# A two-layer retention / mLSTM trunk on one core: rope tables, squares of x and the silu of c placed anew in the opening

## The chip, the core and the metric

The kernel runs on one core of one Trainium2 chip. The core has five engines that run their own lists of instructions in order: TensorE (PE, matrix products; its weight loads are listed apart as PEld), VectorE (DVE), ScalarE (ACT), GpSimd (POOL) and SyncE (SP), which here only issues loads. Sixteen DMA engines move data for the queues that SP, ACT and POOL feed. The metric is the device time of one launch in microseconds (us); the kernel before took 1474.69 us, the median of three runs (1473.51 to 1475.45).

## The reference, cut to what matters

Sequence length 512, width 1024, batch 1, two layers. Layer 0 mixes tokens by retention with 4 heads, layer 1 by an mLSTM; each is followed by a ConvFFN. What the change touches is the beginning of layer 0: silu of c, the modulation vectors, the first RMSNorm, and the rotary tables that q and k need.

```python
def rmsnorm(x, g):
    xf = x.astype(jnp.float32)
    xn = xf * lax.rsqrt(jnp.mean(xf * xf, axis=-1, keepdims=True) + EPS)
    return xn.astype(x.dtype) * g

def rope(t, positions):
    d = t.shape[-1]
    inv_freq = ROPE_BASE ** (-jnp.arange(0, d, 2, dtype=jnp.float32) / d)
    ang = positions.astype(jnp.float32)[..., None] * inv_freq
    cos = jnp.cos(ang)[:, :, None, :].astype(t.dtype)
    sin = jnp.sin(ang)[:, :, None, :].astype(t.dtype)
    ...

c_act = jax.nn.silu(c)
for i in range(DEPTH):
    mod = c_act @ ada_w[i] + ada_b[i]
    sh_t, sc_t, gt_t, sh_f, sc_f, gt_f = [m[:, None, :] for m in jnp.split(mod, 6, axis=-1)]
    h = rmsnorm(x, norm_tok_g[i]) * (1.0 + sc_t) + sh_t
    ...  # retention or mLSTM of h, its gate, then the ConvFFN with sh_f, sc_f, gt_f
```

## The kernel before

x lies transposed: eight tiles x[0] to x[7] of 128 features by 512 tokens, 256 KB each. All products are float32 made of two parts each: an operand is split into a high part (`whi`, `hh`: a copy that TensorE reads at its fast format) and a low part (`wlo`, `hl`: what is left), and a product is high by high, high by low and low by high.

**The opening** is the function `ret_start`. Its tasks, in the names that the profile shows:

- `c_row` is c as one row; ACT takes its silu; TensorE spreads it to all 128 partitions (`pc`), and two copies write it to `c_ext`. Each modulation column is one instruction on DVE, the function `gemv`: a 128x1025 product-and-sum of a loaded tile `ada` (512.5 KB) with `c_ext`. Column KT+k is the scale, column k the shift of tile k.
- Each x[m] is squared into `sq`; the squares are added up on DVE; the function `means` lets four narrow products per group (`pms` from `sq` and `ones_d`) turn the sums into mean squares of tokens. ACT takes the root into `rc`, DVE the reciprocal, and four products with the unit matrix `eye` spread it to a 128x512 tile.
- For each k from 0 to 7: `scaled` writes `xr` on DVE, ACT writes the high part `hh`, DVE the low part `hl`, and `products(k)` runs 24 products of 128x512 of that tile with the first weight chunk `raw` of `w_s` number k (512 KB; the first head's values and gate), whose high part `whi` ACT copies and whose low part `wlo` DVE subtracts (for k of 5 and more ACT and a POOL transfer make it). For tile 0 `xr` and `hh` are made in two halves.
- Products whose result nobody reads keep TensorE at work while it would wait: `busy(n)` issues n of 128x512 on a constant tile `warm`, `alive(m, w)` one on x[m]. Their counts are the constants `BUSY`, `EXTRA` and `ALIVE`.
- `rope_tables` makes cos and sin from the positions (`posi`: one row of 2 KB, read into all 128 partitions) by some 30 operations on DVE over 128x512 (`ra`, `rk`, `rr`, `rn`) and three on ACT. They are first needed when head 0's q and k are rotated.

**What sets the order.** All instructions are first collected by the class `Plan`. Those issued with `plan.pin` set keep the order of the code on their engine: the opening does, up to the loop over k. All others are listed by a planner that goes by estimated durations, due times counted back from TensorE's list, and the state of the buffers; `plan.soon` gives due times by hand (`ROPE_DUE` is 200), and `.after` or `plan.behind` holds an instruction behind another. The result is a fixed list per engine. A change of the opening therefore also reorders what the planner lists behind it. Loads of SP go out in list order; a load also waits until the buffer it writes and one of eight completion counters are free.

Weights, their parts and the `ada` tiles share 18 buffers of 128x1088, two more take `ada` tiles beside them.

After the loop over k come 96 products `pp` for head 0's q and k, then folded products `p`, scores `psc`, and so on to the end; in these the planner keeps TensorE fed.

## Time and profile before

| | before |
|---|---|
| median of 3 runs | 1474.69 us (1473.51 to 1475.45) |
| profiled execution | 1474.7 us, which is its span from the first to the last instruction |
| TensorE busy | 1458.4 us, 99% of the span |
| VectorE busy | 1289.8 us, 87% |
| ScalarE busy | 1063.3 us, 72% |
| TensorE's mean granted clock | 0.994 of full speed |
| first product that is used (`products(0)`) | 21.06 us after the span's start |

The page gives busy time per engine and the granted clock in 40 slices; the timeline lists instructions in order of time, neighbours of one kind merged, with the start, the time that the row covers, and in brackets the idle time before it and what ended it; the stretches give busy time, clock and DMA rate between two moments. Every number is from one execution, and the timeline's zero is its first instruction. A product on float32 operands shows as two records, so the eight narrow products show as x16.

### The profile page before, as it was taken

To read this page: it belongs to the slowest core of one execution; us is meant where nothing else is said; L and a number is where in the kernel's file an instruction comes from. 1 tells how busy PE (TensorE), PEld (TensorE's weight loads), DVE (VectorE), ACT (ScalarE), POOL (GpSimd) and SP (SyncE) were. 2 spreads that over 40 slices of the span, in tenths; PEclk is the share of its full clock that TensorE was granted. 3 is DMA by queue.
4 is the path that set the end of the run, shared out by engine and by line. 5 is a ranking of instruction groups with operands and counts; after the bars stand their busy time and mean duration, and the time that the engine had idled before them with its cause. 6 is when DMAs were issued, how large, how long until landed. Compare 5 with 4: busy or idle time off the path is not lost.

```text
span 1474.7 us, 27429 instructions
## 1 busy us (share of the span) xinstructions
PE 1458.4 (99%) x10564; PEld 1370.7 (93%) x10564; DVE 1289.8 (87%) x2183; ACT 1063.3 (72%) x1604; POOL 244.5 (17%) x279
## 2 busy tenths in 40 slices
PE   8999999999999999999999999999999999999998
PEld 7889999998999999989999998999989999999997
DVE  7899988887998888889897999999989988886866
ACT  5578768786588676666678985988856877667673
POOL 0313112112011111110001321222121011101010
PEclk8999999999999999999999999999999999999999
DMA  9868988988598999799457875888877678568661
GB/s 365 250 165 218 275 232 234 242 251 208 152 223 210 269 266 253 214 236 248 145 176 172 211 207 183 198 194 196 253 190 193 165 183 206 155 168 206 171 162 59
DMA packets 90822, 306.16 MB, mean 208 GB/s; under 512 B 11954, under 2 KB 14514, under 8 KB 90691
## 3 DMA queue, kind: packets, MB, share of 16 engines
q0 software_dynamic: 29520, 106.97, 38.6%
q1 hardware_dynamic: 60882, 197.18, 38.6%
q8 instruction: 82, 1.34, 0.4%
q10 hardware_dynamic: 288, 0.27, 0.1%
q14 instruction: 50, 0.40, 0.1%
HBM read 195.29 MB, written 2.12 MB: 134 GB/s over the span
## 4 chain that ended last, share of the span: by engine, by line
PE 49%; DMA 1%; ACT 1%; DVE 1%; issue 1%; DVEq 0%; POOL 0%; POOLq 0%
PE p L387 20%; PE po L387 16%; PE pv L387 5%; PE pf L387 3%; PE pav L387 2%; DMA wlo<-wt 1%; PE psc L387 1%; ACT whi L387 0%; PE pp L387 0%; ACT mc L387 0%; DVE sl L387 0%; DVE mc L387 0%; ACT wlo L387 0%; ACT L387 0%; DVE ws L387 0%
## 5 line engine op out<-in xcount | busy, mean ns | idle before, releaser
L387 PE MATMUL p<-hh,whi 128*128 128x256 f32 (+1 forms) x1029 | 284.7, 278 | 1.6 <-DVE p L387 1.5
L387 PE MATMUL p<-hl,whi 128*128 128x256 f32 x1024 | 283.6, 277 | 0.0
L387 PE MATMUL p<-hh,wlo 128*128 128x256 f32 x1024 | 281.6, 278 | 0.1
L387 ACT ACTIVATE wlo<-whi 128x1024 fp32r<-128x1024 f32 (+1 forms) x205 | 215.4, 1055 | 25.6 <-PE po L387 14.7
L387 PEld LDWEIGHTS p<-hh,whi 128*128 128x128 f32 x1029 | 193.9, 188 | 3.0 <-DVE p L387 2.4
L387 PEld LDWEIGHTS p<-hl,whi 128*128 128x128 f32 x1024 | 192.5, 188 | 0.4
L387 PEld LDWEIGHTS p<-hh,wlo 128*128 128x128 f32 x1024 | 191.4, 188 | 0.5 <-DMA wlo<-ws 0.3
L387 PE MATMUL p<-t24h,whi 128*128 128x256 f32 x768 | 170.4, 279 | 2.1 <-ACT fs L387 2.1
L387 PE MATMUL po<-ggl,whi 128*128 128x512 f32 (+1 forms) x448 | 153.1, 343 | 0.0
L387 PE MATMUL po<-ggh,whi 128*128 128x512 f32 (+1 forms) x448 | 152.0, 344 | 0.7 <-ACT whi L387 0.7
L387 PE MATMUL po<-ggh,wlo 128*128 128x512 f32 (+1 forms) x448 | 152.5, 343 | 0.0
L387 PE MATMUL p<-t24l,whi 128*128 128x256 f32 x512 | 142.1, 277 | 0.0
L387 DVE SCALAR_TENSOR_TENSOR x<-po,mod,x 128x512 f32<-128x512 f32 (+1 forms) x184 | 113.6, 628 | 30.7 <-PE po L387 29.8
L387 ACT CAST whi<-raw 128x1024 fp32r<-128x1024 f32 (+1 forms) x113 | 113.5, 1015 | 32.6 <-PE po L387 8.4
L387 PEld LDWEIGHTS p<-t24h,whi 128*128 128x128 f32 x768 | 130.4, 188 | 4.9 <-ACT fs L387 2.5
L387 DVE SCALAR_TENSOR_TENSOR cv<-p,vecs,cv 128x511 f32<-128x511 f32 (+1 forms) x152 | 111.2, 743 | 12.0 <-ACT cv L387 11.7
L387 DVE SCALAR_TENSOR_TENSOR ada<-ada,c_ext 128x1025 f32<-128x1025 f32 x96 | 117.6, 1227 | 0.3 <-DMA ada<-ada 0.3
L387 PE MATMUL po<-yl,whi 128*128 128x256 f32 (+1 forms) x352 | 115.3, 328 | 0.0
L387 PE MATMUL po<-yh,whi 128*128 128x256 f32 (+1 forms) x354 | 115.3, 328 | 0.0
L387 PE MATMUL po<-yh,wlo 128*128 128x256 f32 (+1 forms) x352 | 115.3, 328 | 0.0
L387 POOL DMA_DIRECT2D wlo<-wa x55 | 47.5, 864 | 366.3 <-ACT wlo L387 207.7
L387 ACT CAST whi<-ws 128x1024 fp32r<-128x1024 f32 x88 | 92.0, 1048 | 20.7 <-DVE ws L387 13.6
(292 smaller groups left out, 4394.6 us busy)
## 6 DMA issues: line engine op xcount, KB each, us to landing
ada<-ada SPq DMA_DIRECT2D x96, 512.5 KB, 6.6
wlo<-ws POOLq DMA_DIRECT2D x61, 512.0 KB, 7.6
wlo<-wa POOLq DMA_DIRECT2D x55, 512.0 KB, 6.5
wlo<-wt POOLq DMA_DIRECT2D x45, 512.0 KB, 7.5
wa<-w_up SPq DMA_DIRECT2D x38, 512.0 KB, 5.6
wb<-w_up SPq DMA_DIRECT2D x38, 512.0 KB, 8.9
wlo<-raw POOLq DMA_DIRECT2D x34, 512.0 KB, 8.2
raw<-w_o SPq DMA_DIRECT2D x32, 512.0 KB, 7.8
```

The lines of the kernel that those rows point to most:

```text
L387: getattr(c.obj, c.name)(*[real(v) for v in c.a], **{key: real(v) for key, v in c.k.items()})
```

## The change

In the opening:

- `posi` is no longer loaded by ACT's queue at the start but by SP's, behind the first `hh`, after the second part of `vecs`. All of `rope_tables` is issued there too; before, its first five operations came ahead of everything else in the opening, and two more before the first `xr`.
- ACT takes the silu of c first, with one table load ahead; the load of the root's table moves behind the last copy to `c_ext`. Both copies to `c_ext` are now ACT's.
- x[0], x[1] and x[6] are squared on DVE, the others on ACT. The means are formed of three groups (tiles 0 to 3, 4 and 5, 6 and 7) instead of two, so DVE adds five times instead of six.
- Unread products: 7 before the first wait, one on each of x[1], x[3], x[4], x[5], x[6], then 2, 3 and 4 on `warm`, in place of 6, four on x, 4, 3 and 6.
- On SP the first weight chunk goes ahead of the second `ada` tile, and the second ahead of the fourth.

```diff
-BUSY = (6, 1, 1)
-EXTRA = (4, 2, 5)
-ALIVE = (0, 0, 256, 256, 256, 256, 0, 0)
-SUMMED = 6
+FILLS = (7, 2, 3, 4)
...
-    A.dma_start(posi[:], pos.broadcast_to([P, T]))
...
-        plan.soon, tables = ROPE_DUE, rope_tables()
-        next(tables)
-        plan.soon, plan.pin = None, uid("pin")
+        plan.pin = uid("pin")
         A.activation(rc[:, :1], eps_t[:], AF.Silu)
         A.activation(c_row[:1, :], c_row[:1, :], AF.Silu)
-        A.activation(rc[:, :1], eps_t[:], AF.Sqrt)
-        busy(BUSY[0])
-        for i in range(2):
-            PE.matmul(pcs[i][:], one, c_row[:1, i * T : i * T + T], start=True, stop=True)
...
         load_ada(KT)
+        load_raw(0)
         load_ada(0)
-        load_raw(0)
         load_ada(KT + 1)
+        load_raw(1)
         load_ada(1)
-        load_raw(1)
...
+        busy(FILLS[0])
+        square(0, "DVE")
+        square(1, "DVE")
+        square(2)
+        add(0, 1)
+        alive(1, 256)
+        for i in range(2):
+            PE.matmul(pcs[i][:], one, c_row[:1, i * T : i * T + T], start=True, stop=True)
+        square(3)
+        add(1, 2)
+        alive(3, 256)
+        square(4)
+        alive(4, 256)
+        add(2, 3)
+        square(5)
+        means(3, True)
         A.copy(c_ext[:, :T], pcs[0][:])
+        add(4, 5)
+        alive(5, 256)
+        square(6, "DVE")
+        alive(6, 256)
+        means(5, False)
+        square(7)
+        add(6, 7)
+        A.copy(c_ext[:, T : 2 * T], pcs[1][:])
+        busy(FILLS[1])
+        means(7, False)
+        A.activation(rs[:, :1], eps_t[:], AF.Sqrt)
+        busy(FILLS[2])
         gemv(0, KT, mod[KT])
         gain(0, 0, 0)
         A.activation(rc[:, :4], ps[:, :4], AF.Sqrt, bias=eps_t[:])
         high(0)
         V.reciprocal(rc[:, :4], rc[:, :4])
...
+        gemv(0, 0, mod[0])
+        busy(FILLS[3])
         xr = xrs[0] = slot("xr")
...
         S.dma_start(vecs[:, VEC["nffn"] :], vec[:, VEC["nffn"] :]).after = first
+        S.dma_start(posi[:], pos.broadcast_to([P, T])).after = first
+        plan.soon, plan.behind = ROPE_DUE, first
+        for _ in rope_tables():
+            pass
+        plan.soon, plan.behind = None, None
         for k in range(KT):
             ...
                 high(k + 1)
+                plan.calls[-1].after = first
```

TensorE's list from its first product to the first used one (`whi` with `hh`), before:

```order
L387 MATMUL pst_117<-warm_97,ones_81 128x512 x6
L387 MATMUL pc_148<-c_row_99,ones_81 128x512
L387 MATMUL pc_166<-c_row_99,ones_81 128x512
...
L387 MATMUL pst_117<-x_127,ones_81 128x256
L387 MATMUL pst_117<-warm_97,ones_81 128x512 x4
L387 MATMUL pms_211<-ones_d,sq_194 128x1 x4
L387 MATMUL pms_211<-ones_d,sq_200 128x1 x4
L387 MATMUL pst_117<-warm_97,ones_81 128x512 x3
L387 MATMUL pms_211<-eye_134,rc_110 128x128 x4
L387 MATMUL pst_117<-warm_97,ones_81 128x512 x6
L387 MATMUL pst_117<-whi_228,hh_252 128x512
```

and now:

```order
L384 MATMUL pst_115<-warm_97,ones_81 128x512 x7
L384 MATMUL pst_115<-x_110,ones_81 128x256
...
L384 MATMUL pms_199<-ones_d,sq_164 128x1 x4
L384 MATMUL pst_115<-x_125,ones_81 128x256
L384 MATMUL pst_115<-x_129,ones_81 128x256
L384 MATMUL pms_199<-ones_d,sq_178 128x1 x4
L384 MATMUL pst_115<-warm_97,ones_81 128x512 x2
L384 MATMUL pms_199<-ones_d,sq_188 128x1 x4
L384 MATMUL pst_115<-warm_97,ones_81 128x512 x3
L384 MATMUL pms_199<-eye_133,rc_106 128x128 x4
L384 MATMUL pst_115<-warm_97,ones_81 128x512 x4
L384 MATMUL pst_115<-whi_220,hh_238 128x512
```

The means now come in three groups with unread products between them; between the last group and the first used product stand 3, the spread of `rc`, and 4.

ScalarE's list from the root of the means to the high part of tile 1. `whi` is written from the chunks `raw` of `w_s`; `hh_252` and `hh_238` belong to tile 0, `hh_303` and `hh_294` to tile 1. Before:

```order
L387 ACTIVATE rc_110<-pms_211,eps_t 128x4
L387 CAST whi_228<-raw_141 128x1024
L387 CAST whi_238<-raw_154 128x1024
L387 ACTIVATE hh_252<-xr_249,mod_86 128x256 x2
L387 COPY rs_259<-pms_211 128x512
L387 CAST whi_275<-raw_168 128x1024
L387 ACTIVATE hh_303<-xr_295,mod_86 128x512
L387 CAST whi_309<-raw_178 128x1024
```

and now:

```order
L384 ACTIVATE rc_106<-pms_199,eps_t 128x4
L384 CAST whi_220<-raw_138 128x1024
L384 ACTIVATE hh_238<-xr_233,mod_86 128x256 x2
L384 COPY rs_193<-pms_199 128x512
L384 CAST whi_254<-raw_146 128x1024
L384 CAST whi_263<-raw_162 128x1024
L384 CAST whi_276<-raw_174 128x1024
L384 ACTIVATE hh_294<-xr_286,mod_86 128x512
```

Before, three chunks were copied ahead of tile 1's high part; now all of the first four are, the fourth (`raw_174`) directly ahead of it, and none but the first ahead of tile 0's.

SyncE's list between `eye` and the fourth chunk, now:

```order
L384 DMA ada_135<-ada 128x1025
L384 DMA raw_138<-w_s 128x1024
L384 DMA ada_140<-ada 128x1025
L384 DMA ada_144<-ada 128x1025
L384 DMA raw_146<-w_s 128x1024
L384 DMA ada_151<-ada 128x1025
L384 DMA ada_153<-ada 128x1025
L384 DMA ada_160<-ada 128x1025
L384 DMA raw_162<-w_s 128x1024
L384 DMA ada_167<-ada 128x1025
L384 DMA ada_171<-ada 128x1025
L384 DMA raw_174<-w_s 128x1024
```

The fourth chunk was the twelfth of these loads before the change too; only chunks 0 and 1 moved forward by one place each.

More of the change, by code (lines that the diff above doesn't have):

```diff
@@ L1686, in alive, with square @@
         def alive(m, w):
-            if w:
-                PE.matmul(pss[0][:, :w], ones["1"][:].bitcast(F32), x[m][:, :w], start=True, stop=True,
-                          skip_group_check=True)
-        square(0)
-        A.copy(c_ext[:, :T], pcs[0][:])
-        V.tensor_copy(c_ext[:, T : 2 * T], pcs[1][:])
-        for m in range(1, KT):
-            square(m)
-            if m != SUMMED:
-                add(m - 1, m)
-            else:
-                busy(EXTRA[0], free=EXTRA[0])
-                means(m - 1, True)
-            alive(m, ALIVE[m])
-        means(KT - 1, False)
+            PE.matmul(pss[0][:, :w], ones["1"][:].bitcast(F32), x[m][:, :w], start=True, stop=True,
+                      skip_group_check=True)
+        def square(m, eng="ACT"):
+            sq[m] = slot("sq")
+            if eng == "ACT":
+                A.activation(sq[m][:], x[m][:], AF.Square)
+            else:
+                V.tensor_tensor(sq[m][:], x[m][:], x[m][:], op=ALU.mult)
+        busy(FILLS[0])
[14 more added lines that the diff above has]
+        means(3, True)
+        A.copy(c_ext[:, :T], pcs[0][:])
+        add(4, 5)
[10 more added lines that the diff above has]
+        busy(FILLS[2])
         gemv(0, KT, mod[KT])
@@ L1707, in ret_start @@
         V.reciprocal(rc[:, :4], rc[:, :4])
-        pin, plan.pin, plan.soon, plan.behind = plan.pin, None, ROPE_DUE, len(plan.calls) - 1
-        for _ in tables:
-            pass
-        plan.pin, plan.soon, plan.behind = pin, None, None
-        gemv(0, 0, mod[0])
-        busy(BUSY[1] + EXTRA[1], free=EXTRA[1])
         for t in range(4):
```

5 lines of the change are left out of this document (2 added, 3 removed).

## The prediction

> **What bounds the kernel now.** I read the page first: the engines' shares and the granted clock, then the timeline of the first 30 us by engine, then the stretches and the DMA queues.
>
> ```profile
> span 1474.7 us, 27429 instructions
> PE 1458.4 (99%) x10564; PEld 1370.7 (93%) x10564; DVE 1289.8 (87%) x2183; ACT 1063.3 (72%) x1604; POOL 244.5 (17%) x279
> PEclk8999999999999999999999999999999999999999
> ```
>
> TensorE is busy all the time and at full clock but in the first slice. What an opening can give is therefore the distance to the first used product, and only as far as TensorE stays fed from there. The timeline of that distance:
>
> ```profile
> 1.31 2.93 PE L387 MATMUL pst<-warm,ones 128*128 128x512 f32 x6 [1.31 <-POOL warm L387]
> 4.17 1.98 PE L387 MATMUL pc<-c_row,ones 1*128 1x512 f32 x4
> 7.68 3.60 PE L387 MATMUL pst<-x,ones 128*128 128x256 f32 x8 [1.52 <-DMA x<-xT]
> 13.09 2.42 PE L387 MATMUL pms<-ones_d,sq 128*128 128x1 f32 x16 [0.88 <-DVE sq L387]
> 16.80 1.91 PE L387 MATMUL pms<-eye,rc 128*128 128x128 f32 x8
> 20.64 1.16 PEld L387 LDWEIGHTS pst<-whi,hh 128*128 128x128 f32 x4
> 21.06 1.16 PE L387 MATMUL pst<-whi,hh 128*128 128x512 f32 x4
> 26.59 1.07 PE L387 MATMUL pst<-whi,hh 128*128 128x512 f32 x4
> ```
>
> The means end at 15.51, tile 0's products start at 21.06, tile 1's at 26.59: one tile takes 5.53 us. From there TensorE runs without a gap for 62 us:
>
> ```profile
> 26.60:89.00 62.40, 62.40 (x287) 52.13 (x286) 57.87 (x110) 40.68 (x61) 18.34 (x13) 1.00 0.82 246
> ```
>
> So **26.59 is the moment to beat**, not 21.06. Who feeds tile 1:
>
> ```profile
> 4.10 1.28 ACT L387 ACT_TABLE_LOAD   x1
> 18.69 1.04 ACT L387 CAST whi<-raw 128x1024 fp32r<-128x1024 f32 x1 [1.88 <-DMA raw<-w_s]
> 19.64 0.90 ACT L387 ACTIVATE hh<-xr,mod 128x256 fp32r<-128x256 f32 x2
> 22.46 1.05 ACT L387 CAST whi<-raw 128x1024 fp32r<-128x1024 f32 x1 [1.45 <-DMA raw<-w_s]
> 24.72 0.73 ACT L387 ACTIVATE hh<-xr,mod 128x512 fp32r<-128x512 f32 x1 [1.20 <-DVE xr L387]
> 26.32 1.05 ACT L387 CAST whi<-raw 128x1024 fp32r<-128x1024 f32 x1 [0.88 <-DMA raw<-w_s]
> ```
>
> Three times ACT waits for a chunk of `w_s` to land: number 1 at 18.69, 2 at 22.46, 3 at 26.32. Tile 1's `hh` ran between chunks 2 and 3 and was done at 25.45, 1.1 us early.
>
> **The change part by part.** *Loads of x.* DVE waits for the positions until 6.32, SP cannot issue the last x until they land, and the engines move little meanwhile:
>
> ```profile
> 6.32 0.43 DVE L387 CAST ra<-posi 128x512 f32<-128x512 int32 x1 [4.93 <-DMA posi<-pos]
> 8.56 0.69 DVE L387 COPY c_ext<-pc 128x512 f32<-128x512 f32 x1
> 9.16 4.47 DVE L387 TENSOR_TENSOR sq<-sq,sq 128x512 f32<-128x512 f32 x6
> 17.12 0.69 DVE L387 TENSOR_TENSOR rk<-rk,rk 128x512 f32<-128x512 f32 x1
> 17.84 0.43 DVE L387 TENSOR_SCALAR rk<-rk 128x512 f32<-128x512 f32 x1
> 18.74 0.87 DVE L387 SCALAR_TENSOR_TENSOR xr<-x,gain,pms 128x256 f32<-128x256 f32 x2 [0.47 <-PE pms L387]
> SPq L387 <- DMA posi<-pos: 1.8, 1, 1.8
> DMA packets 539, 0.79 MB, mean 187 GB/s; under 512 B 159, under 2 KB 159, under 8 KB 539
> q1 hardware_dynamic: 276, 0.52, 38.8%
> q10 hardware_dynamic: 263, 0.27, 34.1%
> DMA packets 1011, 1.74 MB, mean 405 GB/s; under 512 B 113, under 2 KB 214, under 8 KB 1011
> ```
>
> The first of the two packet rows is the stretch 1.8 to 6.0 us with its queues below it (q10 is ACT's: `vecs` and the positions), the last row 6.0 to 10.3; the DVE rows between are for the parts below. In 4.2 us 0.79 MB moved; at the later 405 GB/s it would be 1.70 MB. Without the positions at least their own 0.27 MB go, 0.67 us; at most the shortfall goes too, (1.70 - 0.79) / 0.405 = 2.25 us, together 2.9 us. I take 2.2 us, nearer the upper end: the shortfall lasts as long as the positions do, but the first x would still have to ramp up. So each later load lands some 2.2 us earlier, 0.67 to 2.9.
>
> *TensorE to the first used product.* Its list is now dense. From 1.31: 7 fills at 2.93 / 6 = 0.49 us, 3.4; one x product at 3.60 / 4 = 0.90 at half clock or half that, `pc` 1.98, two x products 0.9 to 1.8; so about 8 us. Then three groups of means at 2.42 / 2 = 1.21, two x products, two fills: 5.5 to 7.5 more. The means end at 13.5 to 15.5, against 15.51. From there it took 5.55 us; the copy of chunk 1, which held `hh` from 18.74 + 0.87 / 2 = 19.2 to 19.64, is gone, and the last fills are two fewer, so about 5.0. Squares and sums don't set this: on DVE five sums and three squares at 4.47 / 6 = 0.75 us are 6.0 us, most of it while the x still land. The root's table load (the row at 4.10, 1.28 us) costs nothing either, as it runs on ACT while the last sum and the last means run (0.75 + 1.21, behind two fills). If that cover went, it would add 1.28. The first used product starts at 18.5 to 20.5, say 19.0: 2 us earlier. The 5.53 us of tile 0 are done at 24.5.
>
> *Tile 1.* Here ACT's new list decides. `hh` of tile 1 now stands directly behind the copy of chunk 3, which ACT cannot start before that chunk lands. Chunk 3 is the twelfth load behind `eye` in both lists, so it only gains what x gained: 26.32 - 2.2 = 24.1. The copy hands over 0.95 later (18.69 to 19.64), `hh` takes 0.73, TensorE's weight load follows some 0.1 behind (20.54 to 20.64). Tile 1's products start at 26.32 + 0.95 + 0.73 + 0.1 - 2.2 = **25.9, 0.7 us earlier than 26.59**; with 2.9 it is 25.2, with 0.67 it is 27.4, 0.8 later. Whatever the opening gains beyond that is spent waiting for this chunk: TensorE idles from 24.5 to 25.9. A check by bytes: x, `eye` and the twelve loads are 8.46 MB, 20.9 us at 405 GB/s, from about 2 us on; the chunk cannot land before 23.
>
> *The clock.* A gap in TensorE's work has a price of its own:
>
> ```profile
> 6.00:8.00 2.00, 0.48 (x2) 0.33 (x2) 1.58 (x4) 1.57 (x4) 0.00 (x0) 0.89 1.05 404
> 10.00:12.00 2.00, 2.00 (x8) 1.48 (x6) 1.79 (x3) 1.46 (x3) 0.00 (x0) 0.76 1.06 422
> 12.00:14.00 2.00, 1.12 (x9) 0.92 (x9) 1.90 (x4) 0.00 (x0) 0.00 (x0) 1.00 1.04 424
> 14.00:16.00 2.00, 2.00 (x12) 1.90 (x12) 1.09 (x5) 0.39 (x2) 0.00 (x0) 0.60 1.01 410
> 20.00:22.00 2.00, 2.00 (x7) 1.58 (x7) 2.00 (x4) 1.01 (x3) 0.00 (x0) 0.70 1.03 422
> ```
>
> First number behind the stretch's length is TensorE's busy time, the third from the end the granted clock. Read as steps between 1.0 and 0.5, the clock falls at 7.6, rises at 11.0, falls at 14.4, rises at 21.2: multiples of 3.4 us apart. Both falls follow a gap (1.52 us, 0.88 us) and thin work. Those edges continue at 24.6, 28.0, 31.4. A gap of 1.4 us before tile 1 can cost nothing, one step (half speed for up to 3.4 us, 1.7 lost) or, as from 14.4 to 21.2, two. Bounds 0 and 3.4; I take 0.9, as a fall is about as likely as none. The Trainium skill ("TensorE: Matmul & The Clock Gate", Part 1) has a free-running window of 3413 ns, which the spacing bears out, and advises against idle gaps above about 3.4 us; by that advice alone this gap would cost nothing and the sum would be 0.9 lower, yet here the clock fell after gaps of 1.52 and 0.88 us.
>
> *Rope tables.* Seven operations, five from 6.32 to 8.56 and two from 17.12 to 18.27, 3.4 us together, move from the opening to the stretch where DVE is full:
>
> ```profile
> 50.00:60.00 10.00, 10.00 (x46) 8.29 (x45) 7.20 (x14) 6.10 (x7) 0.86 (x1) 1.00 0.98 291
> 60.00:80.00 20.00, 20.00 (x90) 16.58 (x89) 20.00 (x39) 15.04 (x26) 13.00 (x7) 1.00 0.55 125
> 80.00:100.00 20.00, 18.85 (x131) 17.28 (x130) 20.00 (x41) 15.23 (x28) 2.64 (x3) 1.00 0.73 198
> 83.00 0.63 ACT L387 ACTIVATE rk<-rr 128x512 f32<-128x512 f32 x1 [1.96 <-DVE rr L387]
> 90.06 0.37 ACT L387 COPY fs<-p 128x256 f32<-128x256 f32 x1
> 90.48 0.39 PE L387 MATMUL p<-t24h,whi 128*128 128x256 f32 x1 [1.06 <-ACT fs L387]
> ```
>
> TensorE's one wait there, 1.06 us, hangs on `fs`, 7 us behind the tables' end on ACT. DVE has 2.8 us free between 50 and 60, which hides most of the move. Bounds: -1.06 (the wait vanishes, as fewer copies now stand between the tables and `fs`) and +3.4 (the cover is gone). I take +0.3. The positions themselves, now read at about 27 us, delay the loads behind them by 0.7 to 2.9 us; chunk 3 was copied at 26.32 and is used two tiles after 26.59, at 37.6, and the later ones have the same lead, so nothing.
>
> **Sum**, against the profiled execution's 1474.7, which is the runs' median (1474.69): 1474.7 - 0.7 + 0.9 + 0.3 = **1475.2 us**.
>
> **The rivals.**
> - *The clock holds* through the gap. For it: a gap in the middle of dense work, split by an edge, may leave both sides busy enough. Against it: the two falls above. 1475.2 - 0.9 = 1474.3. The skill's advice would have this one.
> - *x is not faster than its bytes allow*: something other than the positions holds the first loads. For it: the queues' rows show both queues slow in one stretch, not which held which. Against it: the rate doubles once the positions are in. Then tile 1 starts at 27.4, the gap is longer and costs a full step: 1474.7 + 0.8 + 1.7 + 0.3 = 1477.5.
> - *DVE becomes the bound* between 58 and 107 us: the moved 3.4 us find no free time, because DVE's list waits for chunks anyway, and the stretch ends that much later than before in absolute time whatever the opening gave. It decides once the delay exceeds DVE's lead over TensorE there; 83.00 to 90.48 says that lead is thin for `fs` only. 1474.7 + 3.4 = 1478.1, slower.
> - *The change does what it says*: the first product is 3 to 4 us earlier and nothing is given back. That needs chunk 3 to land before 21.5, against the bytes. 1474.7 - 3.5 = 1471.2.
>
> **How the numbers follow.** Forecast 0.55, clock holds 0.20, x not faster 0.10, DVE bound 0.09, full gain 0.06. About 0.2% (2.95 us) is what a measurement of this kernel can tell from no change. Faster by more than that: the last case, 0.06. Slower by more (above 1477.6): the DVE case, half of the third and a tail of two clock steps in the forecast, 0.09 + 0.05 + 0.02 = 0.16. The same: 0.78. The range reaches from 1473.0 (clock holds, full 2.9 us, no wait for `fs`: 1474.7 - 1.4 - 0.3) to 1477.6; the forecast's own is 1473.8 to 1476.8.
>
> **What would show it.** In the changed profile: x squared from before 5 us and the last square before 9.5; the means' last group ended before 15.5; the first used product at 18.5 to 20.5; ACT's fourth copy of `raw` waiting for DMA until about 24, `hh` of tile 1 behind it, a gap on TensorE ended by that `hh`, tile 1 at about 25.9, and a half clock in part of 24 to 32. Wrong it would be if ACT does not wait at that copy, if tile 1 starts before 24, or if TensorE shows new gaps between 60 and 110 us.

## The result, and the profile after

The changed kernel takes 1482.2 us, the median of six runs (1480.6 to 1485.35), against 1475.07 for six runs of the kernel before (1472.9 to 1480.1): ratio 1.0051, 95% interval 1.0037 to 1.0065. **It is slower by 0.5%, and the forecast of 1475.2 with its range of 1473.0 to 1477.6 does not hold it.** The profiled execution took 1485.35 us, the longest of the six; its span is 1483.6, 8.9 more than before.

TensorE's opening, as the timeline of the changed kernel has it:

```profile
1.32 3.35 PE L384 MATMUL pst<-warm,ones 128*128 128x512 f32 x7 [1.32 <-POOL warm L384]
4.50 1.22 PE L384 MATMUL pst<-x,ones 128*128 128x256 f32 x2
5.66 3.78 PE L384 MATMUL pc<-c_row,ones 1*128 1x512 f32 x4
9.37 2.08 PE L384 MATMUL pst<-x,ones 128*128 128x256 f32 x4
11.24 1.71 PE L384 MATMUL pms<-ones_d,sq 128*128 128x1 f32 x8
12.80 2.05 PE L384 MATMUL pst<-x,ones 128*128 128x256 f32 x4
14.65 1.71 PE L384 MATMUL pms<-ones_d,sq 128*128 128x1 f32 x8
16.22 1.20 PE L384 MATMUL pst<-warm,ones 128*128 128x512 f32 x2
17.22 1.70 PE L384 MATMUL pms<-ones_d,sq 128*128 128x1 f32 x8
23.62 1.54 PE L384 MATMUL pst<-whi,hh 128*128 128x512 f32 x4
29.55 1.07 PE L384 MATMUL pst<-whi,hh 128*128 128x512 f32 x4
```

There is no gap from 1.32 on. The durations tell the clock: `pc` takes 3.78 us for the same two products (four records) that took 1.98 before, a group of means 1.71, and the first four products of use 1.54 against 1.07 for the next such four. TensorE ran at half clock until some 24.6 us: such a row of four takes 2.08 us at half clock (lean_hand, below) and 1.07 at full, so 1.54 means that the first 0.9 us of it were at half. (The profile's row of granted clocks has nothing to show there, since its records begin with the first change of the clock.) Tile 1 starts at 29.55 instead of 26.59: 3.0 us late.

Nobody else is late. DVE's last sum of squares and ACT's root, in the same kernel:

```profile
3.73 1.44 DVE L384 TENSOR_TENSOR sq<-x 128x512 f32<-128x512 f32 x2 [2.34 <-DMA x<-xT]
10.11 0.69 DVE L384 TENSOR_TENSOR sq<-sq,sq 128x512 f32<-128x512 f32 x1
19.31 0.18 DVE L384 RECIPROCAL rc<-rc 128x4 f32<-128x4 f32 x1 [6.88 <-ACT rc L384]
19.02 0.26 ACT L384 ACTIVATE rc<-pms,eps_t 128x4 f32<-128x4 f32 x1 [7.03 <-PE pms L384]
23.94 2.95 ACT L384 CAST whi<-raw 128x1024 fp32r<-128x1024 f32 x3
28.13 0.72 ACT L384 ACTIVATE hh<-xr,mod 128x512 fp32r<-128x512 f32 x1 [1.24 <-DVE xr L384]
```

The sums are done at 10.80 us, 2.8 earlier than before (13.6), and then DVE and ACT wait 7 us for TensorE's means. The three chunk copies run back to back, without a wait for a load.

The other part of the loss lies far behind the opening. TensorE's busy time by stretches, first the kernel before, then the changed one:

```profile
85.00:150.00 65.00, 63.85 (x500) 62.03 (x499) 61.71 (x106) 51.34 (x87) 16.92 (x23) 1.00 0.81 203
150.00:250.00 100.00, 99.51 (x740) 94.53 (x740) 88.39 (x135) 72.78 (x110) 20.16 (x22) 1.00 0.96 259
250.00:300.00 50.00, 50.00 (x409) 48.87 (x408) 42.97 (x70) 40.51 (x62) 10.13 (x12) 1.00 0.77 200
300.00:340.00 40.00, 38.93 (x283) 36.70 (x282) 34.51 (x58) 32.33 (x52) 5.72 (x12) 1.00 0.83 237
```

```profile
85.00:150.00 65.00, 63.45 (x480) 60.79 (x479) 62.30 (x108) 49.56 (x83) 15.98 (x20) 1.00 0.77 192
150.00:250.00 100.00, 98.49 (x724) 93.07 (x723) 90.21 (x136) 72.78 (x113) 19.88 (x24) 1.00 0.94 252
250.00:300.00 50.00, 49.56 (x404) 48.85 (x404) 39.14 (x62) 38.30 (x58) 10.15 (x11) 1.00 0.86 224
300.00:340.00 40.00, 36.95 (x284) 35.88 (x283) 31.41 (x50) 29.37 (x47) 6.52 (x12) 0.96 0.88 240
314.60:318.00 3.40, 3.40 (x16) 3.40 (x17) 3.31 (x6) 1.43 (x3) 0.33 (x1) 0.52 1.03 339
```

Length less busy time is TensorE's idle time. Before it is 1.15 + 0.49 + 0 + 1.07 = 2.7 us, after 1.55 + 1.51 + 0.44 + 3.05 = 6.55: 3.8 more. The last row shows in addition 3.4 us at half clock, right behind the longest wait, 1.7 us lost. So 3.0 + 3.8 + 1.7 = 8.5 of the 8.9.

The same can be read off one product. The first `po` behind the `pav` products near 340 us stands behind the place where TensorE's lists agree again; in the kernel before, in the change, and in after_again, a second profile of the change:

```profile
341.30 0.39 PE L387 MATMUL po<-yh,whi 128*128 128x512 f32 x1
351.53 0.39 PE L384 MATMUL po<-yh,whi 128*128 128x512 f32 x1
348.40 0.39 PE L384 MATMUL po<-yh,whi 128*128 128x512 f32 x1
```

It is 10.2 and 7.1 us late, which is 7.3 and 7.0 more than tile 1 is (3.0 and 0.1). So the stretch between costs some 1.8 us more than idle time and half clock account for (5.5 and 5.2); where these lie the profiles do not say. Behind this product TensorE's list is the same in all kernels below, and yet the rest took 1123 to 1129 us in their profiles. That 8.5 comes so near to 8.9 is in part chance: the change had made good 1.4 us of its 10.2 at the last product.

The longest of the waits, on TensorE and on ACT's list:

```profile
312.16 0.28 PE L384 MATMUL p<-hh,wlo 128*128 128x256 f32 x1
314.59 0.48 PE L384 MATMUL p<-t24h,whi 128*128 128x256 f32 x1 [2.15 <-ACT fs L384]
312.70 1.06 ACT L384 ACTIVATE wlo<-whi 128x1024 fp32r<-128x1024 f32 x1 [1.59 <-PE p L384]
313.66 0.60 ACT L384 CAST whi<-wb 128x512 fp32r<-128x512 f32 x1
314.17 0.36 ACT L384 COPY fs<-p 128x256 f32<-128x256 f32 x1
```

TensorE needs the copy `fs` before it may go on, and in ACT's list that copy now stands behind a `wlo` that waits for TensorE to free its buffer, and behind a cast. The angle tables were long done by then (their last operation on DVE starts at 87.2 us). What is left of their move at 300 us is the order that the planner found after it: TensorE's list differs from that of before up to some 290 us, ACT's to some 370.

### The profile page after: what moved, and what is told of

Read it like the earlier page. It is cut to its first block, busy times and chain, and to the rows that moved or that the text cites. A ratio compares the mean times of both kernels' runs of the same rounds, so it can differ in the third digit from the quotient of the medians.

```text
span 1483.6 us, 27429 instructions
## 1 busy us (share of the span) xinstructions
PE 1466.1 (99%) x10571; PEld 1375.9 (93%) x10571; DVE 1292.1 (87%) x2184; ACT 1061.5 (72%) x1602; POOL 236.3 (16%) x279
## 4 chain that ended last, share of the span: by engine, by line
PE 83%; DVE 5%; DMA 5%; ACT 3%; issue 2%; POOL 0%; DVEq 0%; POOLq 0%; ACTq 0%
PE p L384 35%; PE po L384 26%; PE pv L384 7%; PE pav L384 4%; PE pst L384 3%; PE pf L384 3%; DMA wlo<-wt 2%; DMA wlo<-wa 2%; PE pp L384 2%; PE psc L384 2%; ACT whi L384 1%; PE pc L384 1%; DVE ws L384 1%; DMA wb<-w_up 1%; DMA wlo<-ws 1%
```

## The experiments

Theory A: two causes that add, TensorE's own opening list and the lists re-planned behind it. Rivals: B, the tables' place alone; C, the opening alone; D, DVE's full stretch at 70 to 106 us sets its own end. "Idle" is TensorE's idle time from 85 to 340 us, and "`po` late" how much later than before the `po` product starts, both as above and from each kernel's one profiled execution. None of them leaves out anything that the output needs.

"Of before" holds for TensorE's list from the first used product on. On ACT and DVE a few instructions still stand in another place up to some 80 us, so that "instruction for instruction" in the expectation of tables_early is not quite so: before, DVE's `rr` at 52.93 us stands ahead of `xr` at 53.53; in tables_early it is behind it, 60.72 and 60.06. Only delay_only has every list of before.

| kernel | lists behind the opening | tile 1 at | `po` late | idle | ratio to before (95%) |
|---|---|---|---|---|---|
| before | its own | 26.59 | | 2.7 | |
| the change | re-planned | 29.55 | 10.2 | 6.55, half clock 3.4 us | 1.0051 (1.0037 to 1.0065) |
| after_again (the change) | the same | 26.69 | 7.1 | 6.2, half clock 3.4 us | 1.0052 (1.0034 to 1.0070) |
| ten_fills | the same | 26.84 | 7.0 | 6.6 | 1.0060 (1.0042 to 1.0077) |
| after_fs | the same but two | 27.08 | 4.8 | 5.25 | 1.0053 (1.0037 to 1.0069) |
| tables_late | re-planned otherwise | 28.40 | 3.5 | 4.4 | 1.0023 (1.0012 to 1.0034) |
| lean | re-planned otherwise | 23.27 | 2.6 | 6.0, half clock 3.4 us | 1.0010 (0.9998 to 1.0023) |
| tables_early | of before | 31.82 | 5.4 | 2.9 | 1.0029 (1.0018 to 1.0039) |
| after_idle | of before | 32.17 | 5.4 | 2.3 | 1.0032 (1.0018 to 1.0046) |
| after_hand | of before | 29.27 | 4.2 | 2.8 | 1.0032 (1.0017 to 1.0046) |
| after_hand_late | of before but five | 28.02 | 9.7 | 2.8 | 1.0032 (1.0018 to 1.0046) |
| lean_idle | of before | 31.63 | 4.1 | 1.8 | 1.0043 (1.0030 to 1.0056) |
| lean_five_late | of before but five | 29.29 | 5.7 | 4.9 | 1.0042 (1.0026 to 1.0058) |
| lean_idle_few | of before | 30.20 | 3.1 | 2.0 | 1.0030 (1.0014 to 1.0045) |
| lean_hand | of before | 27.78 | 3.9 | 2.1 | 1.0034 (1.0021 to 1.0048) |
| lean_hand_hh | of before but three | 25.23 | 6.6 | 1.85 | 1.0053 (1.0039 to 1.0067) |
| delay_only | of before | 28.14 | 1.1 | 2.2 | 1.0007 (0.9996 to 1.0019) |

**tables_early: the changed opening with the tables where they stood.**

Against the changed kernel:

```diff
     A.dma_start(vecs[:, : VEC["nffn"]], vec[:, : VEC["nffn"]])
+    A.dma_start(posi[:], pos.broadcast_to([P, T]))
...
-        plan.pin = uid("pin")
+        plan.soon, tables = ROPE_DUE, rope_tables()
+        next(tables)
+        plan.soon, plan.pin = None, uid("pin")
...
         V.reciprocal(rc[:, :4], rc[:, :4])
+        pin, plan.pin, plan.soon, plan.behind = plan.pin, None, ROPE_DUE, len(plan.calls) - 1
+        for _ in tables:
+            pass
+        plan.pin, plan.soon, plan.behind = pin, None, None
...
-        S.dma_start(posi[:], pos.broadcast_to([P, T])).after = first
-        plan.soon, plan.behind = ROPE_DUE, first
-        for _ in rope_tables():
-            pass
-        plan.soon, plan.behind = None, None
```

> The changed opening, but the positions load on ACT's queue and the angle tables stand where they stood before; behind the opening every engine's list is then the list of before, instruction for instruction. Theory A (two causes: TensorE's own opening list, which ran at half clock until 24.5 us in the changed profile and put tile 1 at 29.55 instead of 26.59, and the lists behind the opening, re-planned by the moved tables, which cost the rest between 150 and 330 us): tile 1 again at 29 to 31 us, half clock up to there, no added waits of TensorE from 90 to 330 us beyond the 2.1 us for fs and 0.4 us for p of before; 1475.1 + 3 to 4 = 1478 to 1479. Rival B (the tables' place alone costs it all): tile 1 near 26.6, time 1475. Rival C (the opening's delay costs it all, and what stood behind it in the profile was chance): 1481 to 1482.

1480.45 us, ratio 1.0029: 4.3 over before (2.7 to 5.8), a little more than A's 3 to 4 and under the 6 to 7 that C asked for. B is out: the tables stood in their old place. Tile 1 came at 31.82, 2.3 later than in the change, because the loads of x come late again; the idle time, 2.9, is that of the old lists, as A has it, and `po` is 5.4 late where tile 1 was 5.2: nearly nothing is added between.

**tables_late: only positions and tables moved.**

Against the kernel before (the second half of the tables behind the reciprocal is taken out likewise):

```diff
-    A.dma_start(posi[:], pos.broadcast_to([P, T]))
-        plan.soon, tables = ROPE_DUE, rope_tables()
-        next(tables)
...
+        S.dma_start(posi[:], pos.broadcast_to([P, T])).after = first
+        plan.soon, plan.behind = ROPE_DUE, first
+        for _ in rope_tables():
+            pass
+        plan.soon, plan.behind = None, None
```

> The kernel before, with only the positions' load and the angle tables moved to behind tile 0, as in the change; squares, silu order, groups of means and fills as before. Theory A: x lands about 2 us earlier, TensorE's opening list stays the old one, so tile 1 is no later than 26.6, perhaps 1 to 2 us earlier if ACT does not wait for a chunk; but the lists behind the opening are re-planned (TensorE's up to about 320 us) and cost some 4 us there: 1477 to 1479 if tile 1 stays, 1476 at best. Rival B (tables' place costs it all): 1480 to 1482. Rival C (only the opening costs): 1473 to 1475.

1479.12 us, 3.4 over before (1.8 to 5.0), at A's upper end; B asked for 1480 to 1482, C for 1473 to 1475. The profile shows how the early loads are wasted in that opening:

```profile
4.18 2.19 PE L387 MATMUL pc<-c_row,ones 1*128 1x512 f32 x4
10.94 1.95 PE L387 MATMUL pms<-ones_d,sq 128*128 128x1 f32 x16 [1.27 <-DVE sq L387]
20.79 2.08 PE L387 MATMUL pst<-whi,hh 128*128 128x512 f32 x4 [4.75 <-ACT hh L387]
```

The means end at 12.9, 2.6 earlier than before. But the planner changed the opening too: on DVE a third modulation column now stands ahead of `xr` (before, it stood behind it, at 20.66) and waits 3.99 us for its load, TensorE idles 4.75 us, and then the first products run at half clock (2.08 for four): tile 1 is 1.8 us later than before, and the re-planned lists add 4.4 - 2.7 = 1.7 of idle time. Together 3.5, as `po` has it, and near the 3.4 of the times.

**lean and ten_fills: less and more on TensorE's opening list.**

Against the changed kernel; in lean the other four calls of `alive` go too. First lean, then ten_fills:

```diff
-FILLS = (7, 2, 3, 4)
+FILLS = (7, 0, 3, 4)
...
-        alive(1, 256)
```

```diff
-FILLS = (7, 2, 3, 4)
+FILLS = (10, 2, 3, 4)
```

> The changed kernel without the ten products on x that nothing reads and without the two fills between the means' second and third group; first fills 7, later ones 3 and 4 as in the change. The lists behind the opening are re-planned once more. Theory A: the last sum is done at 10.8 us as in the changed profile, the last means right behind it at about 11.7, and with the 4.7 us from there to the first product of use this starts at 16 to 17 us, 7 us earlier than in the change; half clock for one more stretch of 3.4 us costs 1.7, tile 1 at 23 to 25. Then 1482.2 - 5 to -6 = 1476 to 1477 if the lists behind the opening cost the same, and whatever is under 1475 shows that they do not. Rival L (loads or DVE set the opening, not TensorE's list): first product not before 21, tile 1 not before 27, 1480 or more.

> The changed kernel with 10 fills instead of 7 at the start; every other instruction of every engine is the same, in the same order. Asks whether the half clock is what makes TensorE's list late, or the list's length. Half-clock theory: three more fills (1.5 us) fill the stretch in which the clock is decided, full clock comes for at least one 3.4 us stretch before 15 us, the rows of pc, x and means shrink to half there, first product of use at 22 to 23.6, time 1481 to 1482. Length theory: no full clock before 24, first product at 25, time 1483.5 to 1484.

lean took 1477.06 us. Its opening, in the timeline:

```profile
4.44 1.98 PE L384 MATMUL pc<-c_row,ones 1*128 1x512 f32 x4
7.73 5.34 PE L384 MATMUL pms<-ones_d,sq 128*128 128x1 f32 x24 [1.32 <-DVE sq L384]
17.78 1.12 PE L384 MATMUL pst<-whi,hh 128*128 128x512 f32 x4
23.27 1.09 PE L384 MATMUL pst<-whi,hh 128*128 128x512 f32 x4
```

Five unread products on x (ten records in the timeline; the expectation counts these) and two fills fewer, and the first product of use is 5.8 us earlier than in the change's profile: TensorE's list set the opening, not loads, DVE or ACT. Part of that is the clock, since `pc` took 1.98 us here; lean_hand, below, had its `pc` at 3.78 as the change had, and its first product at 18.13. Of the 3.3 us that tile 1 is ahead of the kernel before nothing is left, since idle time of 6.0 us and one fall of the clock follow (-3.3 + 3.3 + 1.7 = 1.7; measured +1.4 in the medians, 1.5 by the ratio, -0.3 to 3.4).

In ten_fills the profile and the times disagree. In the profiled execution, the shortest of its six runs (1482.1), the half-clock theory holds: `pc` 2.36, first product of use at 21.36, 2.3 us earlier than in the changed kernel's profile in spite of three more fills. Its median of 1484.42 is 2 us over the change, as the length theory has it. after_again, below, shows that one and the same list can have either clock. Whether more fills bring the full clock more often is not shown, and by its interval ten_fills can't be told from the change.

**after_idle, lean_idle, lean_five_late, lean_idle_few: positions in the opening's idle time, first attempt.**

Against the changed kernel (after_idle) or against lean (the other three); the second half of the tables stands behind the reciprocal, as in tables_early.

```diff
         load_raw(1)
+        S.dma_start(posi[:], pos.broadcast_to([P, T]))
...
+        tables = rope_tables()
+        next(tables)
         gemv(0, KT, mod[KT])
```

In lean_five_late five of the seven operations are then moved in the finished list, ahead of the next angle operation; lean_idle_few has fewer fills:

```diff
-FILLS = (7, 0, 3, 4)
+FILLS = (7, 0, 1, 2)
```

> The whole changed opening (its squares, silu order, three groups of means, products on x that nothing reads, fills), but the positions are read on SP behind the second chunk of w_s, and the first seven angle operations stand in the stretch of the opening in which DVE waits for the means (12.2 to 19.3 us in the changed profile). Behind the opening all lists are those of before. Theory A (two causes that add): the opening's price stays, tile 1 at 29 to 30 us, and the price of the re-planned lists goes; the waits of TensorE between 200 and 330 us are back at before's 0.5 and 1.1 us; 1475.6 + 3 = 1478 to 1479, 3 to 4 under the change. Rival C (the opening alone costs): 1481 to 1482.

> As the run before, but without the ten unread products on x and without the two fills ahead of the means' last group. Theory A: tile 1 at 23.3 to 24, 3 us earlier than before, with the lists of before behind it; whatever of that survives the stretch in which DVE is full (70 to 106 us) is the gain: 1472.3 if all of it, 1474.5 if DVE's list there ends as late as before. Rival D (DVE's full stretch and the loads set its end whatever the opening gives): 1475 to 1476, no gain. In either case 2 to 4 under the run lean, which differs in the place of the tables alone.

> As lean_idle, but five of the seven angle operations (0.43 + 0.89 + 0.69 + 0.43 = 2.4 us of DVE) are taken out of the opening and put directly ahead of the next angle operation, at some 50 us; no other instruction changes its place on any engine. Separates DVE's work from the re-planned lists. DVE theory (what the moved tables cost is DVE's time in its full stretch): 1.5 to 2.4 over lean_idle, with new waits of TensorE between 80 and 110 us. Lists theory (the cost is in the order that the planner then finds, above all between 200 and 340 us): within 0.7 of lean_idle.

> As lean_idle, with one fill instead of three ahead of the rc broadcast and two instead of four ahead of the first product of use. In the profile of lean the broadcast could start at 13.7 and starts at 14.37, and hh is there 0.3 us before the last fill ends; so the first product comes 0.7 to 1.1 us earlier if the fills are what it waits for. Against that the clock: fewer fills may leave the half clock in place for one stretch of 3.4 us more, 1.7 us lost. By the first 0.5 to 1 under lean_idle, by the second 0.7 to 1 over it.

These failed as openings, through an error of mine. DVE's timeline of lean_idle:

```profile
17.81 0.43 DVE L384 CAST ra<-posi 128x512 f32<-128x512 int32 x1 [6.43 <-DMA posi<-pos]
21.46 0.17 DVE L384 RECIPROCAL rc<-rc 128x4 f32<-128x4 f32 x1
```

Issued at 9.33 on SP, the positions landed 8.3 us later, behind everything that SP had issued; the cast waits for them, the reciprocal stands behind the cast, and tile 1 comes at 29 to 32 us. lean_idle_few, 0.5 under lean_idle in the medians, says nothing of fills for the same reason. What they do tell: with the old lists the idle time is 1.8 to 2.3 us however late TensorE is. lean_five_late is the exception. TensorE is 2.3 us earlier there than in lean_idle, and 1.42 us of idle time appear in 85 to 150, most of it one wait of 1.29 for `fs` at 94 us: in the old order five late operations of DVE do cost TensorE time in that stretch, as the DVE theory has it (after_hand, below, where TensorE is as late and two operations are, has 0.12 there). The two medians (1480.4, 1480.76) are alike, so what DVE's work costs in time is not settled.

**after_hand, after_hand_late, lean_hand: second attempt.** Planned as after_idle and lean_idle; then a few instructions are moved in the finished list, and nothing else: the positions on SP ahead of the first chunk, two angle operations ahead of the reciprocal, three ahead of `xr`, two ahead of the next angle operation (in after_hand_late five there).

```diff
-        for n in self.order():
+        out = self.order()
+        for late, ahead in self.moves:
+            out = [n for n in out if n not in late]
+            at = min(out.index(n) for n in ahead)
+            out[at:at] = late
+        for n in out:
```

> What after_idle was meant to be: the positions landed there at 17.6 us, 8.3 after their issue, and the reciprocal stood behind their first operation on DVE. Now the whole changed opening, the positions read on SP ahead of the first chunk of w_s, two angle operations between gain and the reciprocal, three behind the second gemv, two directly ahead of the next angle operation at some 50 us; every list behind the opening is that of before. Theory A (the opening costs 3 us, the lists re-planned for the late tables the other 4): tile 1 at 29.5 to 30.2, no wait over 1.1 us between 200 and 330 us, 1475 + 3 = 1478. Theory C (the opening alone): 1481 to 1482.

> As after_hand, but five of the seven angle operations (2.4 us of DVE) directly ahead of the next angle operation at some 50 us, all else in its place. DVE theory: DVE's full stretch from 70 to 106 us ends 2.4 later, TensorE was already 3 late there and waits for what is left: 0.5 to 2.4 over after_hand. Lists theory: the same as after_hand within 0.7, and so 3 under the change.

> The same places of positions and angle operations and the lists of before, with the opening of lean (no unread products, no fills ahead of the means' last group). Tile 1 at 23.3 to 24, some 3 us earlier than before. Theory D (DVE's full stretch sets its own end): TensorE's wait for fs at 90 us grows from 1.1 to 3 or 4 us, and nothing is left of the gain at 106 us; 1474.5 to 1475.5. Theory A without that bound: 1472 to 1473.

after_hand has the opening of the change (tile 1 at 29.27) and the idle time of before (2.8). It took 1480.37 us, ratio 1.0032: 4.7 over before (2.5 to 6.8), between A's 3 and C's 6 to 7, and its interval overlaps the change's. `po` is 4.2 late, 1.5 more than tile 1, against 7 more in the change. after_hand_late measured the same 1.0032; in its profile TensorE waits 4.61 us for `hh` at 60 us, which I had not meant, so it says nothing of DVE.

lean_hand missed its expectation (tile 1 at 23.3 to 24), and so tests neither of its theories, but it shows the gate that the prediction described: ACT's copy of a chunk that has not landed, with `hh` of tile 1 behind it. ACT's and TensorE's timelines:

```profile
22.27 1.05 ACT L389 CAST whi<-raw 128x1024 fp32r<-128x1024 f32 x1 [2.37 <-DMA raw<-w_s]
26.06 1.04 ACT L389 CAST whi<-raw 128x1024 fp32r<-128x1024 f32 x1 [2.73 <-DMA raw<-w_s]
27.01 0.72 ACT L389 ACTIVATE hh<-xr,mod 128x512 fp32r<-128x512 f32 x1
27.78 2.08 PE L389 MATMUL pst<-whi,hh 128*128 128x512 f32 x4 [3.89 <-ACT hh L389]
```

The opening was early (first product at 18.13), ACT stood at the fourth chunk's copy until the chunk landed, `hh` of tile 1 behind it, TensorE idled 3.89 us and then ran at half clock. So an early opening with ACT's copies in that order (and here the positions' 256 KB ahead of the chunks) is given back to the loads: `po` is 3.9 late, the time 5.0 over before.

**delay_only, after_again, lean_hand_hh.**

delay_only against the kernel before, then lean_hand_hh against lean_hand (a minus puts the copies behind `hh` of that tile):

```diff
-EXTRA = (4, 2, 5)
+EXTRA = (4, 2, 18)
```

```diff
+        plan.moves += [([copies[2], copies[3]], [-his[1]]), ([copies[4]], [-his[2]])]
```

> The kernel before with 13 more fills on TensorE ahead of the first product of use; every list is otherwise that of before. At full clock a fill takes 0.23 us, so tile 1 comes 3 us late, as in the change (29.55 against 26.59), by itself. If a late opening arrives at the end in full: 1475 + 3 = 1478. If TensorE's waits of before at 80 to 106 us (1.15 us) take a part of it: 1477. If the old lists turn a delay into more than itself (as after_hand's 1480 would have it): 1479.5 to 1480.5.

> The changed kernel as it is, to have it beside delay_only on one chip: 1482 (it was 1.0051 of before, 1.0037 to 1.0065). The profile tells whether TensorE's waits of 200 to 330 us (0.5, 0.35, 0.36, 0.44, 2.15, 0.91) are the same in another execution, as a fixed list would make them; and whether the fall of the clock behind the 2.15 us is.

> As lean_hand, but ACT's copies of chunks 2 and 3 stand behind hh of tile 1 and that of chunk 4 behind hh of tile 2 (in lean_hand ACT stood 2.37 and 2.73 us on those chunks' loads, with hh of tile 1 queued behind). Tile 1 at 23.3 to 24 with the old lists. Theory D (DVE's full stretch from 70 to 106 us sets its own end): TensorE waits 3 to 4 us more there, and the end is that of before, 1474.5 to 1476; without that bound 1472.

delay_only: tile 1 at 28.14, 1.55 late and not 3: the 19 fills ahead of it took 5.84 us at nearly full clock, where the 6 of before took 2.91 at half. 1476.67 us, ratio 1.0007 (0.9996 to 1.0019): 1.0 over before, -0.6 to 2.8. How much of the 1.55 arrives, or whether it arrives larger by half as the third case has it (2.3 to 2.8), the times cannot say. In the profile nothing is added: TensorE's wait of 1.06 for `fs` at 90 us is gone, which takes up most of the delay, other waits come in its place, and `po` is 1.1 late.

Its list up to the fills is that of before, and here that list met the half clock:

```profile
4.17 3.78 PE L387 MATMUL pc<-c_row,ones 1*128 1x512 f32 x4
13.19 1.95 PE L387 MATMUL pms<-ones_d,sq 128*128 128x1 f32 x16
```

The means start at 13.19 all the same, against 13.09 in the profile before. There the old list waits 1.52 us for x and 0.88 for a sum, and such waits take up slow products; the new list has none (22.68 us busy of the 22.70 from 1.30 to 24.00), so slow products delay it in full.

after_again is the change's second profile, and it settles most. TensorE's opening, and two stretches of it:

```profile
1.31 3.35 PE L384 MATMUL pst<-warm,ones 128*128 128x512 f32 x7 [1.31 <-POOL warm L384]
5.39 1.98 PE L384 MATMUL pc<-c_row,ones 1*128 1x512 f32 x4
8.29 1.71 PE L384 MATMUL pms<-ones_d,sq 128*128 128x1 f32 x8
14.27 1.70 PE L384 MATMUL pms<-ones_d,sq 128*128 128x1 f32 x8
20.67 1.65 PE L384 MATMUL pst<-whi,hh 128*128 128x512 f32 x4
26.69 1.19 PE L384 MATMUL pst<-whi,hh 128*128 128x512 f32 x4
```

```profile
4.90:8.30 3.40, 3.40 (x11) 1.70 (x12) 2.58 (x4) 2.02 (x4) 0.00 (x0) 0.99 0.97 354
8.40:11.80 3.40, 3.40 (x15) 3.04 (x13) 2.65 (x4) 3.10 (x5) 0.00 (x0) 0.50 1.01 396
```

Same list, same start, but here one stretch of 3.4 us (4.9 to 8.3) was granted full clock, and then half again. That one stretch takes `pc` from 3.78 to 1.98 us and tile 1 from 29.55 to 26.69, level with the kernel before. **The price of the changed opening is 0.1 us in one execution and 3.0 in the other, by the clock's chance.** The waits behind it are the same to 0.01 us in both executions (0.93 and 0.6 near 100 us, 0.5, 0.35 and 0.36 near 215, 0.44, 2.15 and 0.91 between 285 and 330; only one of 0.3 for a load at 155 comes once), and in ten_fills, which has the same list, the 2.15 comes a third time: they belong to the list. The clock fell behind the 2.15 in the two executions of the change and held in ten_fills.

In after_again the sum is 0.1 + 3.5 + 1.7 = 5.3 and `po` is 7.1 late, but its span is only 3.5 over the span before. Behind 340 us TensorE's idle time is 2.4 against 2.7; what else made that part some 3.6 us shorter I did not find. In the change's first profile it was 1.4 shorter, so between executions of one kernel it differs by some 2 us.

lean_hand_hh says nothing of D: tile 1 came at 25.23, but by 60 us TensorE had waited 1.54 and 4.52 us for `hh` behind the copies of later chunks. I had moved the gate on, not taken it away.

**after_fs: the largest wait taken away.**

3043 is `wlo`, 3045 the cast, 3044 POOL's transfer into `wlo`, 2945 the copy `fs`.

```diff
-        for n in self.order():
+        out = self.order()
+        late = [3043, 3045, 3044]
+        out = [n for n in out if n not in late]
+        at = out.index(2945) + 1
+        for n in out[:at] + late + out[at:]:
```

> The changed kernel, but at 312.7 us two operations of ACT (wlo from whi, 1.06 us, which waits for TensorE to free its buffer, and a cast of 0.60) and the POOL transfer that adds to the first stand behind the copy fs that TensorE waits for, instead of ahead of it. fs then waits only for DVE's qkl (done at 312.8) and TensorE goes on at some 313.2 instead of 314.59. Lists theory: the wait falls from 2.15 to 0.7 us, and the clock, which fell to half for 3.4 us behind it in both profiles of the change, either stays (3.1 us gained in all, 1482.4 to 1479.3) or falls as before (1.4 gained, 1481). If TensorE goes on and the next wait takes the gain (the cast is then late): 1482.4 as before.

ACT's timeline of after_fs, and TensorE's stretch from 300 to 340 us:

```profile
310.34 0.37 ACT L388 COPY fs<-p 128x256 f32<-128x256 f32 x1 [2.05 <-DVE pv L388]
310.61 1.06 ACT L388 ACTIVATE wlo<-whi 128x1024 fp32r<-128x1024 f32 x1
```

```profile
300.00:340.00 40.00, 37.95 (x282) 35.70 (x281) 33.86 (x56) 31.99 (x53) 7.34 (x12) 1.00 0.86 244
```

The wait fell from 2.15 to 1.15 us (0.7 was expected), the clock held, the idle time fell from 6.2 to 5.25, and `po` is 4.8 late where the change's list had 7.0 to 10.2: where it acts, the move does what the theory says. The time does not confirm it. 1481.17 us is 1.0 and 1.6 under the two medians of the change, but the kernel before ran at 1474.16 beside it, and the ratio, 1.0053 (1.0037 to 1.0069), is the change's own. A gain of 1 to 3 us is not to be told apart here.

## Why the prediction was wrong

**Loads of x: right.** 2.2 us earlier was forecast, up to 2.9; a load of x takes 3.3 us from issue to landing in the median, against 5.4. x is squared from 3.73 on, and the sums end 2.8 earlier, one addition fewer (0.75) included.

**TensorE to the first used product: the first step that failed.** I took the rows of the profile before at their clock: `pc` 1.98, a group of means 1.21, x products "0.90 at half clock or half that", fills 0.49. The fills were at half clock, `pc` was at full, and "about 8 us" took the lower end of its own figures (1.31 + 3.4 + 0.9 + 1.98 + 1.8 = 9.4). Those rows were themselves a mixture, since before the clock was full in two stretches of the opening. With half clock throughout, the new list from 1.32 to the means' end is 3.35 + 1.22 + 3.78 + 2.08 + 1.71 + 2.05 + 1.71 + 1.20 + 1.70 = 18.8 us, 17.6 where the rows overlap, and ends at 18.9, not at 13.5 to 15.5; the first used product starts at 23.62, not at 19.0. In the luckier execution they are 16.0 and 20.67, still behind the forecast. I had weighed the clock behind a gap at tile 1 and not in the list itself, whose thin products (one column, or one row) did not keep the clock up, and which, unlike the old one, waits for nothing that could hide them.

**The gate: described rightly, for a case that did not come.** Since TensorE was late, ACT did not wait at the fourth copy, and `hh` of tile 1 waited for DVE's `xr`. lean_hand has the gate with its 3.89 us and the half clock behind it.

**The rope tables: the second step that failed, and the larger.** +0.3, between -1.06 and +3.4, was looked for at 58 to 107 us. There the forecast is nearly met (idle 1.55 against 1.15 in 85 to 150). But the planner orders everything behind by due times and free buffers; the moved tables changed TensorE's list up to some 290 us and ACT's to some 370, and the new order costs 0.49 to 1.51, 0 to 0.44 and 1.07 to 3.05 us of idle time in three stretches, with a fall of the clock on top: 3.8 + 1.7 = 5.5 (by `po`, 7.0 to 7.3). The difference of the lists was there to be read before the run; I priced the moved work and not the changed order. All kernels with re-planned lists have 4.4 to 6.6 us of idle time in 85 to 340, all with the old lists 1.8 to 2.9 but lean_five_late. From tile 1 to `po`, the change's list adds 6.8 to 7.3 us in three profiles; the lists of tables_late and lean add 1.7 and 5.9; the old lists add -0.9 to 1.5 in tables_early, after_idle, after_hand, lean_idle, lean_idle_few and delay_only (in the other four a long wait for `hh`, half clock or five late operations of DVE come in between).

**Positions on SP at 27 us: right**, nothing waited for them; and the root's table load was hidden, as said.

**The rivals.** None had it. The DVE case comes nearest in size (+3.4) but has the wrong place, and "x not faster" the right sign for a wrong reason.

How the 7.5 us of the ratio divide is known in part. By the profiles it is 5.2 to 5.5 from the lists (7.0 to 7.3 by `po`) and 0.1 to 3.0 from the opening. By the times, the changed opening with the old lists (tables_early, after_idle, after_hand) costs 4.3 to 4.7 and leaves about 3 for the lists, with intervals of 2 us on each side, and in two of the three that opening is later than the change's. Which it is stays open. That both are there the profiles show; by the times alone the lists' share is not shown, since the intervals of the change (1.0037 to 1.0065) and of after_hand (1.0017 to 1.0046) overlap. No kernel tried is faster than the one before; lean and delay_only are level with it.

## What to carry to other kernels

Where a planner sets the order, a moved block is not priced by its own instructions: compare the lists to where they agree again, and count every wait in that stretch as open. Price a list of short, thin products at half clock throughout as well, and not only at the clock at which the same rows happened to run elsewhere. And work put on TensorE to keep its clock up is itself on the path once the loads behind it are early: five unread products on x and two fills cost the first product 2.9 us where the clock was raised once (20.67 against 17.78) and 5.5 where it was not (23.62 against 18.13).

## What the runs showed of the hardware

The same list from the same start (1.31, 1.32 us) got one stretch of 3.4 us of full clock in one execution and none in another, with 3 us between them. The Trainium skill ("TensorE: Matmul & The Clock Gate", Part 1) says that the window of 3413 ns runs freely and does not start with the kernel, so that the number of slow products varies with the phase; these two profiles agree. The seven fills last 3.35 us, less than that window, so how much of one they cover is chance. They need not fill it: before, six fills of 2.93 us were followed by full clock (`pc` 1.98); in delay_only the same six from the same start were not (3.78).

Being busy is not enough to keep the clock: in after_again TensorE was busy for all of 4.90 to 8.30, mostly with products of one row and of 256 columns, and the stretch behind it was at 0.50.

A gap does not have one price: behind 2.15 us on the same list the clock fell for 3.4 us in two executions and held in a third; it fell behind 1.82 us in lean and held behind 1.63 in tables_late. Where the gap lies between the clock's steps may decide: in the change the clock rose at 24.6 us and fell at 314.7, 85 steps of 3.413 us later, just behind a gap that lies within the last step (312.4 to 314.6), and in after_again likewise (21.9, 312.0, 309.3 to 311.5); 85 steps from the rise at 21.2 in ten_fills end at 311.3, within the gap (310.8 to 313.0), which is so divided between two steps. That is worked out from few gaps, and no run varies it.

The positions, 256 KB broadcast from one row, took 5.1 us to land from ACT's own queue before, and 8.3 us from SP's queue in lean_idle, behind what SP had issued ahead of them.
